# An encoder layer in float32: the vector engine's order of work in the embedding stage and at the end

## The chip, the cores and the metric

The kernel runs on one core of a Trainium2 chip. The core has a matrix engine (TensorE, PE in the profile; its weight loads are PEld), three engines for elementwise work (VectorE or DVE, ScalarE or ACT, GpSimd or POOL), and SyncE (SP), which here only issues transfers. Each engine takes its own instructions in its own order; semaphores order them against each other. Matrix products land in eight banks of PSUM, which DVE and ACT empty.

The metric is the device time of one execution in microseconds (us). Three runs of the kernel before gave 1199.0, 1199.45 and 1202.47 us; the median is 1199.45 us.

## The reference

One layer of a bidirectional encoder over 1024 tokens of width 1024, all in float32:

```
u      = x @ w_in
mix    = concat(retention(u), windowed_attention(u)) @ w_out
h      = LN1(ALPHA * x + mix)
ffn    = (silu(h @ w_ffn_gate) * (h @ w_ffn_up)) @ w_ffn_down
ple    = p @ w_ple_proj                      # p: 1024 x 256, an embedding per layer
out    = LN2(ALPHA * h + ffn + sigmoid(h @ w_ple_gate) * ple)
```

The part in the middle of this document is the last line's embedding term, sigmoid(h @ w_ple_gate) * ple. The part at the end is the last product of the FFN's down projection and LN2.

## The kernel before

**Products.** A float32 operand is split in two (`split`, line 70): ACT copies its rounded part (line 71), and DVE subtracts that from the operand (line 72). A product is then three matmuls (`mm3c`, lines 763 to 765; `mm3`, lines 77 to 79): high by high, high by low, low by high. The big products are done by the Strassen-Winograd scheme: 2 x 2 blocks of 512, and seven block products on sums and differences of blocks in place of eight. One block product (`product`, line 785) is 4 x 4 x 3 = 48 matmuls into four banks; with `outer` the loop over the contraction index kt is the outer one, so that all four banks are touched in turn from the start; without it, bank after bank is finished.

**The embedding stage.** The left operands of block products 5, 6, 7 and 4 are T1, T2, T3 and T4, which `t_sums` (line 995) makes out of blocks of h that are themselves kept as split pairs (`HB`). Each T has two halves q, of 128 x 1024 elements. For each half, DVE makes the sum in two or three passes in place (`both`: lines 1005, 1006, 1007; `less`: lines 1011, 1012), and `put` splits it by ACT and DVE. T1 and T3 take three passes a half; T2 and T4 two, on top of the one before (T2 is made in T1's buffer, T4 in T2's). `t_sums` returns nine closures, the list `steps`. They are called between the parts of the PE program: steps[0] ahead of block product 2, steps[1] and [2] within it, [3] and [4] behind it, [5] and [6] within product 5, [7] and [8] within product 6. The order of the products is 1, 2, 5, 6, 7, 4, 3.

Product 2 completes four tiles of the first block. Behind each, `embed` (line 1051) takes the product of p with w_ple_proj into a further bank (lines 77 to 79), ACT takes the sigmoid of the gate (line 1058) into one of two buffers `sg`, DVE multiplies it by that bank (line 1059) and adds the result to the token tile (line 1061). The banks of these four small products are used again, in product 5, as its four accumulators Z. Behind product 6 and the ones after it, `add4` (line 1072) adds the finished banks to what was kept.

The order on DVE, ACT and POOL in this stage is the source order as long as `es3` is open; it is closed (line 1110) behind the fourth `embed`. From there to the FFN a planner sets the order on these three engines, by its own estimate of when each instruction could start, and it also moves such free instructions ahead of source-ordered ones. PE and SP keep source order throughout.

**The end.** The down projection is 77 units (`dunits`; ND is 77) of a block row each, by the same scheme; unit k's two operands are loaded and split some ten units ahead (`dload`, `dprep`, called by `ahead`). `d_step(k)` (line 1577) issues unit k's matmuls, empties the banks when a product is complete (`dpost`, line 1480), takes one group from the list `later` (`pop`), and then calls `ahead`. Product 3 of the second part is complete at k = 64. Then seven groups of LN2's steps for token tiles 4 to 7 go into `later`: the sums of squares on ACT (`squares`, line 1413), the power -1/2 on POOL (`rstd`, lines 1428 to 1430, and line 1449), the scaling on ACT (line 1452), gain on DVE (line 1455) and bias by an accumulating transfer (line 1456). They are taken at k = 64 to 70, ahead of the calls of `ahead` that split the operands of the last three units, 74 to 76. At k = 70 product 7 is complete; `addto` (line 1398) takes its banks, and the last product (`tail`, line 1460) goes into the same banks, one token tile after the other. From `ahead(2, 4)` on, all five engines are in source order.

Of the kernel before, what the change touches and what calls it, by code (L numbers as in the profile page):

```python
# [42 lines left out]
def layer(tc, xT, xn, w_first, w_mt, w_rv, w_out, w_pg, w_pe, pT, w_gu, w_dn,  # L43
# [26 lines left out]
    def split(raw, hi, lo):  # L70
        act.activation(hi, raw, AF.Copy)  # L71
        dve.tensor_tensor(lo, raw, hi.bitcast(F32), ALU.subtract)  # L72
# [8 lines left out]
    def behind(ins):  # L81

        tc.add_manual_dep(ins.ins, recent[0], mybir.DependencyInfo(
            mybir.DependencyClass.NoSync, mybir.DependencyReason.DATA), reason="order")
        return ins
# [40 lines left out]
    def big16(shape=(P, 2, 2, S)):  # L126
        return big.tile(list(shape), F32R, tag="H", bufs=4, name=nm("H"))
# [142 lines left out]
    later, side, ticks = [], [], [0]  # L270
# [221 lines left out]
    def span(n):  # L492
        return max(n - 1, 0), min(n + 2, NT)
# [75 lines left out]
    def put(x, o, dst):  # L569
        behind(act.activation(o[:, 0, :], x, AF.Copy))  # L570
        behind(dve.tensor_tensor(o[:, 1, :], x, o[:, 0, :].bitcast(F32), ALU.subtract))
        sp.dma_start(dst, o.bitcast(F32))
# [128 lines left out]
    with tc.manual_schedule(engines={mybir.EngineType.PE}):  # L701
# [19 lines left out]
        Y = lambda hh, k: (r.out, hh, (2 * k, 2 * k + 1))  # L721
# [30 lines left out]
    def ct(shape, tag, bufs=None, dt=F32):  # L752
        return cpool.tile(list(shape), dt, tag=tag, bufs=bufs, name=nm(tag))
# [7 lines left out]
    def mm3c(o, lh, ll, rh, rl, start, stop):  # L761

        pe.matmul(o, lh, rh, start=start, stop=False, skip_group_check=True)  # L763
        pe.matmul(o, lh, rl, start=False, stop=False, skip_group_check=True)  # L764
        pe.matmul(o, ll, rh, start=False, stop=stop, skip_group_check=True)  # L765
# [11 lines left out]
    def operands(k):  # L777
        return [fetched.pop(0) for _ in range(k)]
# [3 lines left out]
    def four(k):  # L782
        return [bank(t) for t in sets[k]]

    def product(p, banks, first, stat, side=(), outer=False):

        w = operands(4)
        for kt in range(4 if outer else 0):
            for k in range(4):
                c = slice(k * P, (k + 1) * P)  # L790
                mm3c(banks[k], stat[:, 0, kt, c], stat[:, 1, kt, c], w[kt][:, 0, :], w[kt][:, 1, :], first and kt == 0, kt == 3)
            if kt < len(side):
                side[kt]()
        for k in range(0 if outer else 4):
            c = slice(k * P, (k + 1) * P)
            for kt in range(4):
                mm3c(banks[k], stat[:, 0, kt, c], stat[:, 1, kt, c], w[kt][:, 0, :], w[kt][:, 1, :], first and kt == 0, kt == 3)
            if k < len(side):
                side[k]()
# [141 lines left out]
    Z = four("b")  # L941
# [21 lines left out]
    es3 = contextlib.ExitStack()  # L963
# [28 lines left out]
    TT = {}  # L992
    arena8 = big16((P, 8, 2, HF // 2)).bitcast(F32).rearrange("p a b c -> p a (b c)")

    def t_sums():

        for n in (1, 2, 3):
            TT[n] = big16((P, 2, 4, HF))
        hi = lambda i, j, c: HB[i, j][:, 0, c, :].bitcast(F32)
        lo = lambda i, j, c: HB[i, j][:, 1, c, :].bitcast(F32)  # L1000
        hold = {}

        def both(x, left, right, c):

            dve.tensor_tensor(x, hi(*left, c), hi(*right, c), ALU.subtract)
            dve.tensor_tensor(x, x, lo(*left, c), ALU.add)
            dve.tensor_tensor(x, x, lo(*right, c), ALU.subtract)

        def less(x, left, c):

            dve.tensor_tensor(x, hi(*left, c), x, ALU.subtract)
            dve.tensor_tensor(x, x, lo(*left, c), ALU.add)

        def put(n, x, c):
            split(x, TT[n][:, 0, c, :], TT[n][:, 1, c, :])

        def step(n, q, parts=(0, 1)):
            c = slice(2 * q, 2 * q + 2)
            if 0 not in parts:
                put(n, hold[q], c)  # L1020
                return
            if n == 1:
                hold[q] = ct([P, 2, HF], "ln", 2)
            x = hold[q] if n != 3 else arena8[:, c, :]
            if n == 3:
                both(x, (1, 1), (0, 1), c)
            elif n == 1:
                both(x, (0, 1), (0, 0), c)
            else:
                less(x, (1, 1) if n == 2 else (1, 0), c)  # L1030
            if n == 4 and q == 0:
                TT[4] = ct([P, 2, 4, HF], "h2", dt=F32R)
            if 1 in parts:
                put(n, x, c)

        return [lambda k=k: [step(1, q, (k,)) for q in range(2)] for k in range(2)] + \
            [lambda k=k: step(2, 0, (k,)) for k in range(2)] + \
            [lambda n=n, q=q: step(n, q) for n, q in ((2, 1), (3, 0), (3, 1), (4, 0), (4, 1))]

    def gate_w(p, kts=range(4)):
        for kt in kts:
            stream(pgd[p - 1, kt])
# [21 lines left out]
    def store_z(upto):  # L1066
        while len(zstores) > upto:
            zstores.pop(0)()
# [20 lines left out]
    for k in range(4, NT):  # L1089
        times_alpha(k)  # L1090
    steps = t_sums()
    steps[0]()
    w2, wpe = operands(4), operands(2)

    def first_tile(k):
        embed(k, 0, X[k], wpe, "to"[k % 2], pt[k])
        if k < 2:
            pt[k + 2] = load_p(k + 2)

    for k in range(4):  # L1100
        c = slice(k * P, (k + 1) * P)
        for kt in range(4):
            mm3c(X[k], HB[1, 0][:, 0, kt, c], HB[1, 0][:, 1, kt, c], w2[kt][:, 0, :], w2[kt][:, 1, :], False, kt == 3)
        if k:
            first_tile(k - 1)
        if k in (1, 2):
            steps[k]()
    gate_w(5, (2, 3))
    first_tile(3)
    es3.close()  # L1110
    for k in range(3, 5):
        steps[k]()
    gate_w(6)
    Z = four("b")
    product(5, Z, True, TT[1], steps[5:7], True)
    store_z(0)
    gate_w(7)
    pt = {t: load_p(t) for t in range(2)}
    Y = four("a")
    product(6, Y, True, TT[2], steps[7:9])  # L1120
    gate_w(4)
    u2 = [arena8[:, 4 + k, :] for k in range(4)]
    add4(u2, s1, Y)
# [157 lines left out]
    n = 0  # L1281
    for k, upto in enumerate((2, 4, 8, 12)):
        c = slice(k * P, (k + 1) * P)
# [95 lines left out]
    accd, R, later = [], [], []  # L1379

    def load_acc():
        accd.append(a_tile([P, D], "acc"))
        sp.dma_start(accd[-1], zd[len(accd) - 1])

    def pop():
        for f in later.pop(0):
            f()
# [172 lines left out]
    NG, ND = len(gunits), len(dunits)  # L1560
# [3 lines left out]
    def ahead(what, upto):  # L1564

        units = gunits if what == 2 else dunits
        while done[what] < min(upto, len(units)):
            units[done[what]][what % 2]()
            done[what] += 1

    def load_ln2():
        for j in range(2):
            g = ct([P, D], "u", 4)
            sp.dma_start(g, lnp[2 + j].partition_broadcast(P))
            ln2.append(g)

    def d_step(k):
        dunits[k][2]()
        dunits[k][3]()
        if later and k < ND - 6:  # L1580
            pop()
        while stores and stores[0][0] <= NG + k:
            stores.pop(0)[1]()
        pa = min(10, 5 + k // 3)
        ahead(0, k + 1 + pa + 4)
        ahead(1, k + 1 + pa)
        if k in (2, 3, 4, 5, 8, 9, 10, 11):
            load_acc()
        if k == ND - 24:
            load_ln2()  # L1590

    ET = mybir.EngineType
    with tc.manual_schedule(engines={ET.PE, ET.DVE, ET.Activation, ET.Pool, ET.SP}):
        ahead(2, 4)
        for k in range(NG):
            gunits[k][1]()
            gunits[k][2]()
            ahead(2, k + 1 + min(8, 4 + k))
            while stores and stores[0][0] <= k:
                stores.pop(0)[1]()  # L1600
            j = k + 1 - NG
            if j == -6:
                arenas_a()
                op_arena(ct([P, 4, 2, HF], "h0a", dt=F32R))
                op_arena(big16((P, 4, 2, HF)))
                op_arena(big16((P, 4, 2, HF)))
                arena("chain", ct([P, 8, HF], "h0b"), 8)
            if j == -4:
                op_arena(big16((P, 4, 2, HF)))
                arena("b", big.tile([P, 8, HF], F32, tag="H", bufs=4, name=nm("H")), 8)  # L1610
            if j >= -6:
                ahead(0, j + 7)
            if j >= -4:
                ahead(1, j + 5)
        arena("chain", ct([P, 8, HF], "h2"), 8)
        op_arena(ct([P, 4, 2, HF], "h3", dt=F32R), 4)
        rings["op"] += [ct([P, 2, HF], "u", 4, F32R) for _ in range(2)]
        for k in range(ND):
            d_step(k)
# [86 lines left out]
```

## Time and profile before

| | |
|---|---|
| median of the runs | 1199.45 us |
| the profiled execution's own time | 1199.99 us |
| its span on the core, first to last instruction | 1198.0 us |
| PE busy | 1181.0 us, 99% of the span, 5892 matmuls |
| DVE busy | 771.5 us, 64% |
| ACT busy | 542.5 us, 45% |
| POOL busy | 363.8 us, 30% |
| granted PE clock, mean | 0.998 |
| embedding stage, products 5, 6 and 7 | from about 486 to 521 us |
| last product's first matmul, last matmul | 1172.5 us, 1188.7 us |

The profile's times count from the span's start. A row of the timeline gives the start, the duration, the engine, the line, the operation, output<-inputs, and the shapes; "x2" is two instructions in one row, and a bracket at the end gives the idle time of the engine before it and what ended it. Matmuls overlap, so a matmul's duration (0.39 us) is longer than the distance to the next. A row of the waits gives the engine and line that waited, for whom, the sum, the count and the longest.

### The profile page before, as it was taken

To read this page: it belongs to the slowest core of one execution; us is meant where nothing else is said; L and a number is where in the kernel's file an instruction comes from. 1 tells how busy PE (TensorE), PEld (TensorE's weight loads), DVE (VectorE), ACT (ScalarE), POOL (GpSimd) and SP (SyncE) were. 2 spreads that over 40 slices of the span, in tenths; PEclk is the share of its full clock that TensorE was granted. 3 is DMA by queue.
4 is the path that set the end of the run, shared out by engine and by line. 5 is a ranking of instruction groups with operands and counts; after the bars stand their busy time and mean duration, and the time that the engine had idled before them with its cause. 6 is when DMAs were issued, how large, how long until landed. Compare 5 with 4: busy or idle time off the path is not lost.

```text
span 1198.0 us, 16664 instructions
## 1 busy us (share of the span) xinstructions
PE 1181.0 (99%) x5892; PEld 983.9 (82%) x5892; DVE 771.5 (64%) x1346; ACT 542.5 (45%) x1046; POOL 363.8 (30%) x342
## 2 busy tenths in 40 slices
PE   9999999999999999999999999999999999999996
PEld 7888888888888888788888888888888888888885
DVE  5654788877767788947744555545554565775668
ACT  5566238676786257203323332333322325562463
POOL 2001020202010022002756465555746342034232
PEclk9999999999999999999999999999999999999999
DMA  6335635434336864666233311332123169999977
GB/s 251 110 136 211 250 120 212 160 123 162 121 126 232 324 232 167 237 219 211 88 123 132 130 64 71 132 132 98 78 88 132 71 202 300 355 276 207 263 182 210
DMA packets 78098, 207.80 MB, mean 173 GB/s; under 512 B 9024, under 2 KB 13248, under 8 KB 78016
## 3 DMA queue, kind: packets, MB, share of 16 engines
q1 hardware_dynamic: 69376, 189.98, 44.0%
q0 software_dynamic: 8640, 16.78, 8.0%
q8 instruction: 46, 0.75, 0.2%
q14 instruction: 36, 0.29, 0.1%
HBM read 139.35 MB, written 62.13 MB: 168 GB/s over the span
## 4 chain that ended last, share of the span: by engine, by line
PE 94%; DVE 3%; ACT 1%; issue 1%; DMA 0%; POOL 0%; DVEq 0%; SPq 0%; ACTq 0%
PE bmm L77 6%; PE bt L763 6%; PE bt L764 6%; PE bt L765 6%; PE bmm L79 6%; PE bmm L78 6%; PE bs L763 6%; PE bs L764 6%; PE bs L765 6%; PE bo L763 5%; PE bo L764 5%; PE bo L765 5%; PE bmm L764 5%; PE bmm L763 5%; PE bmm L765 5%; PE bo L553 2%
## 5 line engine op out<-in xcount | busy, mean ns | idle before, releaser
L77 PE MATMUL bmm<-H,w 128*128 128x512 f32 x240 | 96.8, 403 | 0.4 <-ACT H L71 0.4
L79 PE MATMUL bmm<-H,w 128*128 128x512 f32 x240 | 94.1, 392 | 0.0
L78 PE MATMUL bmm<-H,w 128*128 128x512 f32 x240 | 93.8, 391 | 0.0
L1168 POOL TENSOR_TENSOR H<-ln 128x512 f32<-128x512 f32 x22 | 29.2, 1327 | 180.9 <-DMA ln<-in_w_gu 174.3
L1198 POOL TENSOR_TENSOR ev<-ev 128x512 f32<-128x512 f32 x33 | 54.9, 1664 | 91.2 <-DVE ev L1213 64.2
L72 DVE TENSOR_TENSOR w<-H,w 128x512 fp32r<-128x512 f32 x44 | 39.1, 889 | 63.1 <-ACT w L71 63.1
L72 DVE TENSOR_TENSOR w<-raw,w 128x512 fp32r<-128x512 f32 x56 | 45.3, 810 | 45.7 <-ACT w L71 45.2
L514 POOL COPY sc<-skb 128x1 f32<-128x1 f32 x64 | 13.0, 208 | 188.3 <-PE bt L541 149.4
L1196 ACT ACTIVATE ev<-ev 128x512 f32<-128x512 f32 x33 | 20.9, 632 | 103.5 <-DVE ev L1213 103.5
L1202 POOL TENSOR_TENSOR ev<-ev,ev 128x512 f32<-128x512 f32 x44 | 62.7, 1436 | 2.6
L72 DVE TENSOR_TENSOR u<-H,u 128x512 fp32r<-128x512 f32 x47 | 37.1, 790 | 38.9 <-ACT u L71 38.6
L77 PEld LDWEIGHTS bmm<-H,w 128*128 128x128 f32 x240 | 45.2, 188 | 10.5 <-ACT H L71 1.3
L79 PEld LDWEIGHTS bmm<-H,w 128*128 128x128 f32 x240 | 45.0, 188 | 10.0
L78 PEld LDWEIGHTS bmm<-H,w 128*128 128x128 f32 x240 | 45.1, 188 | 7.7
L71 ACT ACTIVATE u<-H 128x512 fp32r<-128x512 f32 x47 | 29.7, 631 | 43.5 <-PE bt L765 9.0
L523 ACT ACTIVATE sc<-sc,st 128x385 f32<-128x385 f32 (+1 forms) x64 | 37.2, 584 | 25.3 <-DVE st L521 25.2
L519 DVE CUSTOM_DVE_ANT_0 sc<-cst,bs,skb 128x384 f32<-128x384 f32 (+1 forms) x64 | 34.9, 576 | 16.3 <-PE bs L518 15.7
L71 ACT ACTIVATE w<-raw 128x512 fp32r<-128x512 f32 x56 | 34.7, 624 | 17.1 <-PE bo L79 7.0
L475 POOL TENSOR_TENSOR sm<-sm,cst 128x8 f32<-128x8 f32 x8 | 15.6, 1950 | 86.9 <-DVE sm L474 86.9
L874 POOL TENSOR_TENSOR stt<-stt,cst 128x1 f32<-128x1 f32 x8 | 12.1, 1514 | 91.2 <-DVE stt L873 91.2
L1172 POOL TENSOR_TENSOR H<-raw,H 128x512 f32<-128x512 f32 x22 | 37.8, 1718 | 0.0
L71 ACT ACTIVATE w<-H 128x512 fp32r<-128x512 f32 x44 | 27.4, 622 | 21.4 <-PE bs L765 6.3
(802 smaller groups left out, 3822.6 us busy)
## 6 DMA issues: line engine op xcount, KB each, us to landing
ad<-ev SPq DMA_DIRECT2D x33, 512.0 KB, 2.7
pgd<-pro SPq DMA_DIRECT2D x28, 512.0 KB, 2.8
raw<-in_w_gu SPq DMA_DIRECT2D x22, 512.0 KB, 4.3
ln<-in_w_gu SPq DMA_DIRECT2D x22, 512.0 KB, 3.5
raw<-ad SPq DMA_DIRECT2D x40, 256.0 KB, 5.5
ln<-ad SPq DMA_DIRECT2D x37, 256.0 KB, 6.7
H<-in_w_dn SPq DMA_DIRECT2D x33, 256.0 KB, 7.7
wod<-aq SPq DMA_DIRECT2D x15, 512.0 KB, 2.6
```

The lines of the kernel that those rows point to most:

```text
L71: act.activation(hi, raw, AF.Copy)
L72: dve.tensor_tensor(lo, raw, hi.bitcast(F32), ALU.subtract)
L77: pe.matmul(o, lh, rh, start=start, stop=False)
L78: pe.matmul(o, lh, rl, start=False, stop=False)
L79: recent[0] = pe.matmul(o, ll, rh, start=False, stop=stop).ins.name
L523: act.activation(sc[g][:, :nk + 1], sc[g][:, :nk + 1], AF.Exp, bias=st_[:, 1, j, g:g + 1], accum_out=st_[:, 2, j, g:g + 1])
L763: pe.matmul(o, lh, rh, start=start, stop=False, skip_group_check=True)
L764: pe.matmul(o, lh, rl, start=False, stop=False, skip_group_check=True)
L765: pe.matmul(o, ll, rh, start=False, stop=stop, skip_group_check=True)
L1172: pool.tensor_tensor(s[3], a(0, 1), s[0], ALU.subtract)
L1198: pool.tensor_tensor(c[:, 1, :], c[:, 0, :], c[:, 1, :], ALU.mult)
L1202: pool.tensor_tensor(self.ev[dst][:, 0, :], left, right, op)
```

## The change

In the embedding stage the closures of `t_sums` become eight, two for each T: `sums` makes the passes of both halves, `parts` splits both. steps[0] stands where it stood, steps[1] too; T2's sums and splits come behind the fourth `embed`, T3's within product 5, and T4's within product 6. `es3` is closed behind product 6. At the end, `d_step` takes a group of LN2's steps behind its calls of `ahead` for k = 64 to 70, and ahead of them for smaller k as before.

```
-        return [lambda k=k: [step(1, q, (k,)) for q in range(2)] for k in range(2)] + \
-            [lambda k=k: step(2, 0, (k,)) for k in range(2)] + \
-            [lambda n=n, q=q: step(n, q) for n, q in ((2, 1), (3, 0), (3, 1), (4, 0), (4, 1))]
+        return [lambda f=f, n=n: [f(n, q) for q in range(2)] for n in (1, 2, 3, 4) for f in (sums, parts)]
...
-        if k in (1, 2):
-            steps[k]()
+        if k == 1:
+            steps[1]()
     gate_w(5, (2, 3))
     first_tile(3)
-    es3.close()
-    for k in range(3, 5):
+    for k in range(2, 4):
         steps[k]()
     gate_w(6)
     Z = four("b")
-    product(5, Z, True, TT[1], steps[5:7], True)
+    product(5, Z, True, TT[1], steps[4:6], True)
     store_z(0)
     gate_w(7)
     pt = {t: load_p(t) for t in range(2)}
     Y = four("a")
-    product(6, Y, True, TT[2], steps[7:9])
+    product(6, Y, True, TT[2], steps[6:8])
+    es3.close()
...
     def d_step(k):
         dunits[k][2]()
         dunits[k][3]()
-        if later and k < ND - 6:
+        if later and k < ND - 13:
             pop()
         while stores and stores[0][0] <= NG + k:
             stores.pop(0)[1]()
         pa = min(10, 5 + k // 3)
         ahead(0, k + 1 + pa + 4)
         ahead(1, k + 1 + pa)
+        if later and ND - 13 <= k < ND - 6:
+            pop()
```

The orders of PE, SP and POOL are the same in both programs, and so is the number of instructions on each engine. On DVE about thirty instructions of the embedding stage and two pairs at the end stand elsewhere, on ACT five instructions at the end, and the two halves of T2's split change places.

In the changed kernel DVE takes, behind T1's splits: the second, third and fourth multiply and add of `embed`, T2's two passes on the first half and two on the second, T2's two splits, five passes of T3, the first bank of `add4`, T3's sixth pass, T3's first split, the second bank, T3's second split, and T4 with the third and fourth banks between its passes. At the end the splits of unit 75 stand ahead of the sums of squares of tile 5, and those of unit 76 ahead of the scaling of tile 4.

More of the change, by code (lines that the diff above doesn't have):

```diff
@@ L1015, in put, with span, sums @@
             split(x, TT[n][:, 0, c, :], TT[n][:, 1, c, :])
[L1017 to L1021, printed above, removed]
+        def span(q):
+            return slice(2 * q, 2 * q + 2)
+        def sums(n, q):
+            c = span(q)
             if n == 1:
@@ L1030, in step, with parts @@
                 less(x, (1, 1) if n == 2 else (1, 0), c)
+        def parts(n, q):
             if n == 4 and q == 0:
                 TT[4] = ct([P, 2, 4, HF], "h2", dt=F32R)
-            if 1 in parts:
-                put(n, x, c)
-        return [lambda k=k: [step(1, q, (k,)) for q in range(2)] for k in range(2)] + \
-            [lambda k=k: step(2, 0, (k,)) for k in range(2)] + \
-            [lambda n=n, q=q: step(n, q) for n, q in ((2, 1), (3, 0), (3, 1), (4, 0), (4, 1))]
+            put(n, hold[q] if n != 3 else arena8[:, span(q), :], span(q))
+        return [lambda f=f, n=n: [f(n, q) for q in range(2)] for n in (1, 2, 3, 4) for f in (sums, parts)]
     def gate_w(p, kts=range(4)):
```

## The prediction

> **What bounds the kernel now.** First the page, then the waits of PE, then the timelines of PE, DVE, ACT and POOL around the waits that the change can reach. The page's head and the waits of PE:
>
> ```profile
> span 1198.0 us, 16664 instructions
> ...
> PE 1181.0 (99%) x5892; PEld 983.9 (82%) x5892; DVE 771.5 (64%) x1346; ACT 542.5 (45%) x1046; POOL 363.8 (30%) x342
> ...
> PE bmm L763 <- DVE sg L1059: 1.8, 1, 1.8
> ...
> PE bo L763 <- DVE sg L1059: 0.7, 1, 0.7
> PE bs L763 <- DVE acc L1398: 0.6, 1, 0.6
> ```
>
> PE is the bound; only what lets it wait less, or more, changes the time. Three of its waits lie where the edit is: two for the third and fourth multiply of `embed` (line 1059), one for the emptying of a bank ahead of the last product (line 1398). PE in the embedding stage:
>
> ```profile
> 485.49 0.39 PE L79 MATMUL bo<-u,p 128*128 128x512 f32 x1
> 485.71 0.39 PE L763 MATMUL bmm<-w,H 128*128 128x512 f32 x1
> ...
> 488.32 0.50 PE L763 MATMUL bmm<-w,H 128*128 128x512 f32 x1 [1.77 <-DVE sg L1059]
> ...
> 490.65 0.50 PE L763 MATMUL bo<-w,H 128*128 128x512 f32 x1 [0.67 <-DVE sg L1059]
> ...
> 491.45 0.39 PE L763 MATMUL bmm<-u,H 128*128 128x512 f32 x1
> ...
> 499.61 0.39 PE L763 MATMUL bt<-w,H 128*128 128x512 f32 x1
> ...
> 510.49 0.39 PE L763 MATMUL bt<-w,H 128*128 128x512 f32 x1
> ```
>
> Product 5 starts at 485.71, product 6 at 499.61, product 7 at 510.49. The last two are 48 matmuls apart: 10.88 / 48 = 0.2267 us each where nothing waits. Product 5's first 12 matmuls should end at 485.71 + 12 x 0.2267 = 488.43; the thirteenth starts at 491.45. The two waits with their slow restarts cost 3.02 us. What DVE and ACT do then:
>
> ```profile
> 470.94 1.22 DVE L1005 TENSOR_TENSOR ln<-h,h0a 128x1024 f32<-128x1024 f32 x1
> 472.19 1.23 DVE L1006 TENSOR_TENSOR ln<-ln,h 128x1024 f32<-128x1024 f32 x1
> ...
> 481.85 0.68 DVE L1059 TENSOR_TENSOR sg<-sg,bo 128x512 f32<-128x512 f32 x1
> 482.44 1.22 DVE L1011 TENSOR_TENSOR ln<-h,ln 128x1024 f32<-128x1024 f32 x1
> 483.58 0.68 DVE L1061 TENSOR_TENSOR acc<-acc,sg 128x512 f32<-128x512 f32 x1
> ...
> 485.32 2.35 DVE L1012 TENSOR_TENSOR ln<-ln,h 128x1024 f32<-128x1024 f32 x2
> 487.59 0.68 DVE L1059 TENSOR_TENSOR sg<-sg,bmm 128x512 f32<-128x512 f32 x1
> ...
> 484.35 0.60 ACT L1058 ACTIVATE sg<-bs 128x512 f32<-128x512 f32 x1 [3.96 <-DVE acc L1061]
> 486.56 2.19 ACT L71 ACTIVATE H<-ln 128x1024 fp32r<-128x1024 f32 x2 [1.61 <-DVE ln L1012]
> ```
>
> The third multiply starts at 487.59, after four passes of T2 (lines 1011, 1012), though T2 is not wanted before 499.61. The fourth small product's last matmul ends by 485.49 + 0.39 = 485.88; the fourth sigmoid waited for the second add (line 1061), itself behind a T2 pass. Now the end:
>
> ```profile
> 1171.48 0.39 PE L765 MATMUL bmm<-H 128*128 128x512 f32 x1
> 1172.51 0.47 PE L763 MATMUL bs<-H 128*128 128x512 f32 x1 [0.64 <-DVE acc L1398]
> ...
> 1160.49 0.62 ACT L71 ACTIVATE h<-raw 128x512 fp32r<-128x512 f32 x1
> ...
> 1164.37 1.24 ACT L1452 ACTIVATE acc<-acc,stt 128x1024 f32<-128x1024 f32 x1 [0.28 <-POOL stt L1449]
> 1165.52 0.71 ACT L1413 ACTIVATE sg<-acc,stt 128x512 f32<-128x512 f32 x1
> ...
> 1166.93 0.62 ACT L71 ACTIVATE u<-ln 128x512 fp32r<-128x512 f32 x1
> ...
> 1162.70 0.20 DVE L1428 TENSOR_SCALAR stt<-stt 128x1 f32<-128x1 f32 x1
> ...
> 1167.58 0.69 DVE L72 TENSOR_TENSOR u<-ln,u 128x512 fp32r<-128x512 f32 x1 [2.38 <-ACT u L71]
> ...
> 1168.79 1.22 DVE L1455 TENSOR_TENSOR acc<-acc,u 128x1024 f32<-128x1024 f32 x1
> ...
> 1171.68 1.28 DVE L1398 TENSOR_TENSOR acc<-acc,bs 128x512 f32<-128x512 f32 x2
> ...
> 1189.13 0.69 DVE L1398 TENSOR_TENSOR acc<-acc,bmm 128x512 f32<-128x512 f32 x1 [0.18 <-PE bmm L765]
> ...
> 1157.02 0.86 POOL L1340 DMA_DIRECT2D h<-in_w_dn  x1 [0.41 <-DVE H L72]
> 1163.18 0.56 POOL L1430 TENSOR_TENSOR stt<-stt,cst 128x1 f32<-128x1 f32 x1 [5.30 <-DVE stt L1429]
> 1163.82 0.52 POOL L1449 TENSOR_TENSOR stt<-stt 128x1 f32<-128x1 f32 x1
> ...
> 1165.91 0.19 POOL L1449 TENSOR_TENSOR stt<-stt 128x1 f32<-128x1 f32 x1
> ```
>
> Without the wait the last product would start at 1171.48 + 0.23 = 1171.71; it starts at 1172.51, and 0.08 later again by its slow restart (0.47 instead of 0.39). The end is worth 0.88 us at most. After it DVE waits for PE at 1189.13: what PE gains there the end of the span gains.
>
> **The change part by part.** *Third and fourth multiply ahead of T2.* Nothing is added or removed; DVE's order changes. The second multiply stays at 481.85, its add follows at 482.44 + 0.1 (it depends on it), done by 483.2; so the fourth sigmoid can run at about 483.2 (its bank is complete by then: the next small product follows it on PE), done by 483.9 in place of 484.95. The third small product ends about 6 x 0.2267 = 1.36 before the fourth, at 484.5: third multiply 484.6 to 485.3, its add to 486.0, fourth multiply 486.0 to 486.7, its add to 487.4. Product 5 wants the third one's bank for its second accumulator at 485.71 + 3 x 0.2267 = 486.39 and the fourth one's for its fourth at 487.75. Both are there 1.1 us early. PE gains all of the 3.02 us.
>
> *T2 later.* Two passes, then two: the rows of lines 1005 and 1006 are 1.25 apart where one needs the other, the pair on line 1012, independent, 2.35 - 1.22 = 1.13. From 487.3: 1.25 + 1.13 + 1.25 + 1.13 gives 492.1; ACT splits the second half by 492.1 + 1.1 = 493.2, DVE by 494.5. Product 6 now starts at 499.61 - 3.02 = 496.59. Slack 2.1 us, so no cost; all beyond it would be PE's. [...]
>
> *T3 and T4, and the banks between them.* From 494.4, five passes of T3 end at 500.4. Then DVE must take product 6's first bank, complete at 496.59 + 2.72 + 0.2 = 499.5: no wait. Sixth pass, first split, second bank (complete 502.2), second split: 505.1, against product 7 at 510.49 - 3.02 = 507.47. If PE were later here, the banks would be later, but never so late that product 7 waits: the second bank comes half a product ahead of it, and 0.6 + 1.2 us of DVE follow. T4 with banks three and four ends near 513.7, product 4 starts at 518.35. Cost nothing.
>
> *Queues.* ACT holds only the splits here; POOL nothing. SP's order is kept, and its stores of the tiles can go earlier, since the adds do. Product 6's last weights:
>
> ```profile
> 485.91 0.42 SPq L774 DMA_DIRECT2D u<-pgd  x1
> ...
> DMA to landing us min/median/max: 2.6/4.0/7.5
> ```
>
> At the longest landing of these transfers 485.91 + 7.5 = 493.4, ahead of 496.59. From here on every stage is paced by PE or by what PE frees, so I let the 3.02 us travel to the end unshortened.
>
> *The end: splits of units 75 and 76 ahead of LN2's steps.* Same instructions, other order on ACT and DVE. ACT: 0.52 for a split's copy (1160.49 to the next), 1.41 for a pair of squares (1165.52 to 1166.93), 1.15 for a scaling (1164.37 to 1165.52). Unit 74's copies end at 1161.5, unit 75's at 1162.6, squares of tile 5 at 1164.0, unit 76's copies at 1165.1. DVE takes unit 75's halves to 1163.9, and only then tile 4's small steps, 1162.70 before: 1.2 later. POOL then needs 0.56 + 0.52 + gaps: tile 4's scaling starts at 1165.5 in place of 1164.37. But unit 76 is out of the way: scaling to 1166.7, squares of tile 6 to 1168.1, scaling of tile 5 to 1169.3, squares of tile 7 to 1170.7; then DVE's two small steps, and line 1398 at 1171.1 in place of 1171.68. That is 0.6 of the 0.88. Bounds: all of it, 0.88, if a step or two is quicker; below nothing, -0.4, if POOL's steps lose a further microsecond to DVE's splits. I take 0.6, since every step has its own row. Unit 76's accumulating transfer was issued at 1157.02; its copy is now wanted at 1164.5, 7.5 us later:
>
> ```profile
> DMA to landing us min/median/max: 4.5/4.8/7.1
> ```
>
> *Sum.* Span 1198.0 - 3.02 - 0.6 = 1194.4. The profiled execution took 1199.99, so 1.99 lie around the span: 1196.4. The median of the runs is 0.54 below the profiled one: 1195.85, against 1199.45.
>
> **The rivals.** *B: POOL eats the end's gain.* The row at 1163.82 took 0.52, the same step at 1165.91 took 0.19. DVE was subtracting in a split at the first and idle at the second. In the new order tile 4's power follows unit 75's splits and precedes unit 76's by 0.3 us; if DVE gets in first, power and product lose between 0.33 (0.52 - 0.19, one of them) and 0.66 (both), ACT's whole chain slips by some 0.5, and line 1398 is back at 1171.6. Then only 3.02 + 0.1 is left: 1196.3. For it: the two rows; against it: the power should start while DVE waits for ACT. [...]
>
> *C: T2 comes late.* If DVE's chain behind the fourth multiply runs 3.6 us longer than I reckon, PE waits 1.5 at product 6: 1.5 + 0.6 are left, 1197.3. For it: T2 had 7 us of slack and keeps 2.1. Against it: no DVE duration in the rows varies by more than 0.1 us.
>
> *D: slower.* T2 now stands behind two multiplies that wait for PE, ACT and the transfers of p. If the fourth small product is late, PE waits for it in either kernel, but here the sums wait too. From 2.1 us of lateness this costs, from 2.1 + 3.6 = 5.7 the kernel is slower than before, and with 9.3 by 0.3%, 1203. The trace shows no such wait of PE at 484.35 to 485.49, which speaks against it.
>
> **How the numbers follow.** Chances: forecast 0.65, B 0.17, C 0.10, D 0.08. 0.3% is 3.6 us, about what a measurement of this kernel can tell from no change, and the forecast's 3.6 lies on it; its own range is 1195.2 to 1196.6 with the runs' scatter of half a microsecond. I count 0.7 of the forecast and a quarter of B as over 0.3% (0.50), D as slower (0.08), the rest as within (0.42). Range: down to the full 3.9 with 0.9 of scatter below, 1194.6; up past B and most of C, 1198.6.
>
> **What would show it.** Right: no PE wait for line 1059, product 6 starting 10.9 us after product 5, no PE wait on T2 (lines 71, 72) at product 6 or on line 1072 at 7; the third multiply within 0.2 us of its small product's end; the wait for line 1398 at 0.3 or less. Wrong: a PE wait of over half a microsecond at product 6, 7 or 4; new PE waits in the FFN or the down projection, which would mean that the shift is absorbed there; a wait for line 1398 of 0.6 or more (B).

## The result, and the profile after

The changed kernel took 1195.99 us (median of 6 runs, 1194.9 to 1196.8), against 1199.62 us for the kernel before beside it (6 runs). The ratio is 0.9966 with a 95% interval of 0.9953 to 0.9979, so the gain is 3.6 us, 0.2 to 0.5%. The forecast was 1195.85. The profiled span fell from 1198.0 to 1194.4 us, the forecast's own figure.

The head of the page of the changed kernel, and its waits of PE (us in total, times, longest). Line numbers behind the embedding's function are one lower than before: 1059 is now 1058, 1398 is 1397.

```profile
span 1194.4 us, 16665 instructions
...
PE 1180.5 (99%) x5892; PEld 984.2 (82%) x5892; DVE 773.2 (65%) x1346; ACT 542.6 (45%) x1046; POOL 366.3 (31%) x342
...
PE bt L404 <- ACT ptr L543: 1.6, 1, 1.6
...
PE bt L763 <- DMA u<-wod: 0.3, 1, 0.3
PE bs L763 <- DVE acc L1397: 0.2, 1, 0.2
```

The two waits for `embed`'s multiply are gone; the one at the end is 0.2 in place of 0.6; the longest that is left (line 404) lies in an earlier stage. PE has as many instructions as before and as much busy time within 0.5 us: all that changed is what it waits. The timeline of PE in the embedding stage and at the end, changed kernel:

```profile
485.88 0.39 PE L763 MATMUL bmm<-w,H 128*128 128x512 f32 x1
...
496.76 0.39 PE L763 MATMUL bt<-w,H 128*128 128x512 f32 x1
...
507.64 0.39 PE L763 MATMUL bt<-w,H 128*128 128x512 f32 x1
...
518.52 0.39 PE L763 MATMUL bt<-w,h 128*128 128x512 f32 x1
...
1168.37 0.39 PE L765 MATMUL bmm<-H 128*128 128x512 f32 x1
1168.94 0.47 PE L763 MATMUL bs<-H 128*128 128x512 f32 x1 [0.18 <-DVE acc L1397]
```

Products 5, 6, 7 and 4 start 10.88 us apart each: 48 matmuls without a gap. Before, product 6 came 13.90 behind product 5, so the embedding stage gives 3.02 us. At the end PE lost 1168.94 - 1168.37 - 0.23 = 0.34 us, against 1172.51 - 1171.48 - 0.23 = 0.80 before: 0.46 less. The last product starts 1172.51 - 1168.94 = 3.57 earlier: 3.02 and 0.46, and 0.24 for matmuls between 994.65 and 995.34 that were slow in the trace of before alone, less 0.17 by which product 5 starts later (485.88 against 485.71); that makes 3.55, to 0.02.

DVE in the changed kernel, from the second multiply to T3's last split:

```profile
482.02 0.68 DVE L1058 TENSOR_TENSOR sg<-sg,bo 128x512 f32<-128x512 f32 x1
...
484.79 0.69 DVE L1058 TENSOR_TENSOR sg<-sg,bmm 128x512 f32<-128x512 f32 x1 [1.36 <-PE bmm L79]
...
487.48 1.22 DVE L1011 TENSOR_TENSOR ln<-h,ln 128x1024 f32<-128x1024 f32 x1
...
492.27 2.44 DVE L72 TENSOR_TENSOR H<-ln,H 128x1024 fp32r<-128x1024 f32 x2
...
500.67 0.68 DVE L1071 TENSOR_TENSOR H<-raw,bt 128x512 f32<-128x512 f32 x1
...
504.14 1.22 DVE L72 TENSOR_TENSOR H<-H,H 128x1024 fp32r<-128x1024 f32 x1
```

The third multiply now waits for its small product (1.36 us idle, released by line 79), where before it stood behind T2's passes. T2 is ready at 492.27 + 2.44 = 494.71, 2.05 ahead of product 6; T3 at 505.36, 2.28 ahead of product 7.

### The profile page after: what moved, and what is told of

Same layout as the page of the kernel before. It is cut to its first block, busy times and chain, and to the rows that moved or that the text cites. A ratio compares the mean times of both kernels' runs of the same rounds, so it can differ in the third digit from the quotient of the medians.

```text
span 1194.4 us, 16665 instructions
## 1 busy us (share of the span) xinstructions
PE 1180.5 (99%) x5892; PEld 984.2 (82%) x5892; DVE 773.2 (65%) x1346; ACT 542.6 (45%) x1046; POOL 366.3 (31%) x342
## 4 chain that ended last, share of the span: by engine, by line
PE 96%; ACT 1%; DVE 1%; DMA 1%; issue 0%; POOL 0%; SPq 0%; DVEq 0%; ACTq 0%
PE bmm L77 6%; PE bt L763 6%; PE bt L765 6%; PE bt L764 6%; PE bs L763 6%; PE bs L765 6%; PE bs L764 6%; PE bmm L79 6%; PE bmm L78 6%; PE bmm L765 5%; PE bmm L763 5%; PE bo L765 5%; PE bo L763 5%; PE bo L764 5%; PE bmm L764 5%; PE bo L553 2%
```

## The experiments

**The changed kernel once more (e0), and each half alone (e1, e2).** e0 is the changed kernel. e1 has the embedding's edit and `d_step` as before; e2 has `d_step` as changed and the embedding as before:

```
 def d_step(k):                       # e1 against the changed kernel
-        if later and k < ND - 13:
+        if later and k < ND - 6:
             pop()
...
-        if later and ND - 13 <= k < ND - 6:
-            pop()
```

> The changed kernel once more, as the measure for the three kernels beside it. Both theories expect what its first profile showed: 3.6 us less than before, no PE wait in products 5 to 7, and a wait of 0.2 us for line 1397 ahead of the last product.

> The embedding stage's half of the change alone; the end as before. Theory (two separate terms: a bank that DVE gives back in time in product 5, and DVE's chain ahead of the last product): 3.0 us less than before, the PE waits for line 1058 gone, the wait for the bank ahead of the last product at 0.6 us and more, as before. Rival (part of the gain is a shift that the transfer-bound down projection gives to the end): the end's wait shrinks here too, and the gain is nearer 3.6.

> The end's half alone; the embedding stage as before. Theory: 0.4 to 0.6 us less than before, from the wait ahead of the last product, 0.64 to 0.2; the two waits in product 5 stay at 1.8 and 0.7. Rival (the end's order has no effect, POOL's slow steps take it back): 0.0 to 0.1 less, and the wait stays at 0.6.

Measured, each against the kernel before on the same chip (1200.04): e0 1196.67, ratio 0.9974 [0.9963, 0.9984]; e1 1196.41, ratio 0.9973 [0.9961, 0.9985], span 1194.6; e2 1199.99, ratio 1.0000 [0.9991, 1.0008], span 1197.7. The waits of PE in e2:

```profile
PE bmm L763 <- DVE sg L1059: 1.7, 1, 1.7
...
PE bo L763 <- DVE sg L1059: 0.7, 1, 0.7
```

All of the gain that can be measured is the embedding's; the end alone shows none. e1 brought the very numbers of its rival (3.63 us less and no wait at the end). But the rival's reason, a shift given on by the embedding, doesn't fit e2, which has the embedding as before and no wait at the end either. No line of e2's list has the wait for the emptying of the bank. It is missing from e0's too, which has the same order at the end and should have shown 0.2, and from e1's, which has the old one and should have shown 0.6. So whether PE waits there is not a matter of the order of LN2's steps alone.

**The squares ahead (e3).** The groups of LN2's steps are dealt out anew, on top of the changed kernel (q squares, f power, m scaling, w gain and bias; indices 0 to 3 are tiles 4 to 7): tile 7's squares go ahead of tile 5's scaling, and tile 5's gain behind the emptying of the banks:

```
-  [w[0], m[1], q[3], f[2]], [w[1], m[2], f[3]], [m[3]], [w[2], w[3]]
+  [w[0], q[3], f[2], m[1]], [m[2], f[3]], [m[3]], [w[1], w[2], w[3]]
```

> The changed kernel with another order of the last norm steps: the squares of tile 7 ahead of the scaling of tile 5, and DVE's gain pass of tile 5 behind the last product's four bank reads. Theory (what is left of the wait is ACT's chain, scaling, squares, scaling, squares, ahead of DVE's small step for tile 7): line 1397 starts about 1 us earlier, PE's wait there is gone, 0.4 us less than the changed kernel, and POOL's steps for tiles 6 and 7, 1.93 and 1.01 us beside DVE's gain passes, fall towards 0.6 and 0.2. Rival (DVE is late again, now in the last product, because three gain passes stand ahead of it): the same time as the changed kernel, the wait moved to line 1395 or 1434.

Measured: 1196.81, ratio 0.9976 [0.9967, 0.9985], span 1196.8, no better than e0, with a wait of 1.4 us where none was expected. The profiled execution is the slowest of e3's ten (1198.83 us), so such a wait is not in all of them. The timeline of DVE in e3 around the end, then PE's wait:

```profile
1158.40 0.68 DVE L1395 CUSTOM_DVE_ANT_0 acc<-acc,bo 128x512 f32<-128x512 f32 x1
...
1170.14 1.27 DVE L1397 TENSOR_TENSOR acc<-acc,bs 128x512 f32<-128x512 f32 x2
...
1169.21 0.39 PE L765 MATMUL bmm<-H 128*128 128x512 f32 x1
1170.96 0.47 PE L763 MATMUL bs<-H 128*128 128x512 f32 x1 [1.36 <-ACT acc L1451]
```

The work from the first custom pass on the preceding product's banks (line 1395, at 1158.40) to the emptying (1170.14) is a fixed chain on DVE, ACT and POOL: here 11.74 us. The same two rows give its length in every profile. PE restarts 0.82 after the emptying begins (1170.96 - 1170.14). What varies is the lead, the time from that first pass to the moment at which PE would be free for the last product (here 1169.21 + 0.23 - 1158.40 = 11.04). In the kernel before, DVE's first pass of the chain is this row; its emptying (1171.68) and PE's last matmul ahead of it (1171.48) stand in the prediction:

```profile
1158.09 0.68 DVE L1396 CUSTOM_DVE_ANT_0 acc<-acc,bo 128x512 f32<-128x512 f32 x1
```

PE waits where the chain plus 0.82 is longer than the lead (us, from the same rows of each trace; e4 to e8 follow below):

| kernel | order at the end | chain | lead | PE waits |
|---|---|---|---|---|
| before | old | 13.59 | 13.62 | 0.80 |
| e1 | old | 13.60 | 15.15 | 0 |
| after | new | 12.92 | 13.40 | 0.34 |
| e0 | new | 12.94 | 15.39 | 0 |
| e2 | new | 12.92 | 14.92 | 0 |
| e4 | new | 12.92 | 13.97 | 0 |
| e5 | new | 12.93 | 13.49 | 0.26 |
| e6 | new | 12.92 | 12.06 | 1.69 |
| e7 | new | 12.92 | 14.74 | 0 |
| e8 | new | 12.93 | 14.85 | 0 |
| e3 | squares first | 11.74 | 11.04 | 1.52 |

The edit at the end makes the chain 0.67 us shorter each time, and e3's order another 1.18. But the lead varies by 4.3 us between traces, without regard to the order. What starts the chain is seen on ACT ahead of it. The timeline of ACT in e3 and, below it, in e0:

```profile
1157.12 0.63 ACT L71 ACTIVATE H<-h0b 128x512 fp32r<-128x512 f32 x1 [0.55 <-DMA h0b<-in_w_dn]
```

```profile
1151.88 0.63 ACT L71 ACTIVATE H<-h0b 128x512 fp32r<-128x512 f32 x1 [1.15 <-DMA h0b<-in_w_dn]
```

The split just ahead of the chain waits for an accumulating transfer of `w_dn` to land: in all eleven traces it starts 0.104 or 0.105 us after one has landed (e3: landed at 1157.015). With the old order PE needs a lead of 13.59 + 0.83 = 14.42. Six of the eleven traces have less; over all eleven the edit would save 0.35 us on average (0.67 in five, 0.45 in e4, nothing in five), 0.03% of the time. That is below what e2's interval can resolve. Why the transfers land earlier in one run than in another stays open.

**The source order given up, in two places (e4, e5).** `es3.close()` is where the planner takes over. e4 closes it behind `first_tile(3)`, where it stood before, e5 behind T2:

```
     first_tile(3)
+    es3.close()                      # e4
     for k in range(2, 4):
         steps[k]()
+    es3.close()                      # e5
...
     product(6, Y, True, TT[2], steps[6:8])
-    es3.close()                      # both
```

> The changed kernel, but the source order of DVE, ACT and POOL ends behind the fourth embedding tile, where it ended before; the planner then puts three of T2's four passes back between the multiplies and adds. Theory (the bank's multiply must not stand behind sums): the third multiply is just in time, the fourth ends near 488.5, PE wants its bank at 487.9 and waits 0.6 to 0.7 with a slow restart: 0.6 to 0.9 us more than the changed kernel. Rival (the grouping of sums and splits by itself makes the gain): the same time as the changed kernel, no PE wait in product 5.

> The changed kernel, but source order ends behind T2's splits: T3, T4 and the sums of banks are the planner's again, with two T3 and T4 passes in another order. Theory (T3 and T4 have slack, their order is free): the same time as the changed kernel within 0.2 us, no PE wait in products 5 to 7. Rival (source order to the sixth product is part of the gain): 0.5 us or more is lost in product 7 or 4.

Measured: e4 1197.13, ratio 0.9971 [0.9960, 0.9983], span 1194.1; e5 1200.05, ratio 0.9997 [0.9988, 1.0005], span 1198.4. In e4 the planner puts T2's passes between the multiplies again; the third multiply is in time, and PE loses 0.65 us at the fourth one, as expected; the time doesn't show it. The waits of PE in e4, then DVE's emptying of product 6's first bank:

```profile
PE bo L763 <- DVE sg L1058: 0.4, 1, 0.4
```

```profile
504.00 0.68 DVE L1071 TENSOR_TENSOR H<-raw,bt 128x512 f32<-128x512 f32 x1
```

T3, T4 and the banks are the planner's in e4 too, and no later product waits. So 3.02 - 0.65 = 2.4 us of the embedding's gain come without the edit to `es3.close()`. e5 is the miss: I had taken the order of T3 and T4 for free, and the whole gain is lost. DVE and ACT in e5 ahead of product 7:

```profile
498.96 1.22 DVE L1011 TENSOR_TENSOR ln<-h0b,ln 128x1024 f32<-128x1024 f32 x1
...
503.50 1.22 DVE L1012 TENSOR_TENSOR ln<-ln,h0b 128x1024 f32<-128x1024 f32 x1
504.64 1.22 DVE L1011 TENSOR_TENSOR ln<-h0b,ln 128x1024 f32<-128x1024 f32 x1
505.78 1.22 DVE L72 TENSOR_TENSOR H<-H,H 128x1024 fp32r<-128x1024 f32 x1
506.91 1.22 DVE L1012 TENSOR_TENSOR ln<-ln,h0b 128x1024 f32<-128x1024 f32 x1
508.05 1.22 DVE L72 TENSOR_TENSOR h<-ln,h 128x1024 fp32r<-128x1024 f32 x1
509.18 0.68 DVE L1071 TENSOR_TENSOR H<-raw,bt 128x512 f32<-128x512 f32 x1
...
508.16 1.06 ACT L71 ACTIVATE h<-ln 128x1024 fp32r<-128x1024 f32 x1 [2.28 <-DVE ln L1012]
```

T3 is ready in time (last split 505.78 + 1.22 = 507.00). But the planner puts T4's passes (lines 1011, 1012 on `h0b`) among T3's and T4's first split ahead of the emptying of product 6's first bank (line 1071): 509.18, against 500.67 in the changed kernel. Product 7 goes into that bank, and DVE works on sums that nobody wants for 10 us. PE in e5, and below it the windows view (stretch, its length, then busy us and count of PE, weight load, DVE, ACT, POOL, then the granted clock, DMA share and GB/s):

```profile
507.42 0.39 PE L765 MATMUL bs<-u,H 128*128 128x512 f32 x1
509.96 0.47 PE L763 MATMUL bt<-w,H 128*128 128x512 f32 x1 [2.16 <-ACT h L71]
...
511.33 0.63 PE L765 MATMUL bt<-u,H 128*128 128x512 f32 x1
511.76 0.63 PE L763 MATMUL bt<-w,H 128*128 128x512 f32 x1
```

```profile
511.00:514.00 3.00, 3.00 (x9) 2.33 (x8) 1.79 (x3) 0.00 (x0) 0.00 (x0) 0.50 0.71 289
```

The page names ACT's line 71 as releaser. That instruction ended at 509.22 and writes T4, which product 7 doesn't read; the emptying ended at 509.86, and PE starts at 509.96. The wait costs 509.96 - 507.42 - 0.23 = 2.31. A microsecond later the granted clock is 0.50 and matmuls come 0.42 to 0.43 apart for 3.4 us: another 1.60, with 0.10 for the slow restart ahead of it. Together that is the 4.0 us by which e5's span is longer than the changed kernel's. e4 had the planner too, and no such order; so what costs is the order that the planner chose from this point on, not that it chose.

**Extra work ahead of T2 (e6, e7).** Three, or six, additional DVE passes of 128x1024, into a buffer that T3 overwrites later, stand behind `first_tile(3)`; they are work that the kernel doesn't need:

```
     first_tile(3)
+    for k in range(3):               # e6; range(6) in e7
+        dve.tensor_tensor(<T3's buffer>, <high part>, <low part>, ALU.add)
     for k in range(2, 4):
```

> The changed kernel with three further DVE passes of 128 x 1024, into a part that T3's sums overwrite, between the fourth add and T2: T2 comes 3.5 us later. As the prediction had it (slack 2.1 us against product 6's first matmul): PE waits 1.4 us at product 6. Other theory (the first matmul that needs T2's low part is the third, the first that needs its second half the seventh; by the profile the slack is 3.5 and 3.9): 0 to 0.2 us, the same time as the changed kernel within 0.3.

> The same with six passes, T2 7.0 us later. As the prediction had it: 4.9 us of PE waits. Other theory: product 6's third matmul waits 3.3 us for the first half's low part, and T3, which the banks of product 6 now stand between, costs product 7 up to 0.9: 3.3 to 4.5 us more than the changed kernel, so slower than before or equal to it.

Measured: e6 1196.71, ratio 0.9970 [0.9961, 0.9980], no wait of PE in the embedding stage. e7: 1202.44, ratio 1.0017 [1.0008, 1.0026]. DVE and PE in e6, then PE in e7, at the start of product 6:

```profile
487.97 3.49 DVE L1110 TENSOR_TENSOR H<-h0a 128x1024 f32<-128x1024 f32 x3
...
496.17 2.44 DVE L72 TENSOR_TENSOR H<-ln,H 128x1024 fp32r<-128x1024 f32 x2
...
497.25 0.39 PE L763 MATMUL bt<-w,H 128*128 128x512 f32 x1
...
497.70 0.39 PE L765 MATMUL bt<-w,H 128*128 128x512 f32 x1
```

```profile
497.16 0.39 PE L765 MATMUL bo<-u,H 128*128 128x512 f32 x1
498.54 0.50 PE L763 MATMUL bt<-w,H 128*128 128x512 f32 x1 [0.99 <-ACT H L71]
498.88 0.40 PE L764 MATMUL bt<-w,H 128*128 128x512 f32 x1
500.98 0.50 PE L765 MATMUL bt<-w,H 128*128 128x512 f32 x1 [1.71 <-DVE H L72]
...
502.55 0.63 PE L764 MATMUL bt<-w,H 128*128 128x512 f32 x1
```

In e6 T2 is complete at 496.17 + 2.44 = 498.61, 1.36 after product 6 has begun, and nobody waits. e7's two waits tell why: the first two matmuls of a product want only ACT's rounded part of T2 (line 71); the third (line 765) is the first to want DVE's remainder, of the first half alone; the second half comes from the seventh on. So the slack is read at the third matmul. In the changed kernel the remainder of the first half is there at 492.27 + 1.22 = 493.49, the third matmul at 496.76 + 2 x 0.227 = 497.21: 3.7 us. In e6 that remainder is there at 497.39, 0.31 ahead of its matmul at 497.70; three passes fit, just. In e7 the waits cost 1.15 + 1.87 us, and again the clock drops, for another 1.60. So e7 took 5.7 us more than e6, where 3.3 to 4.5 more than the changed kernel were expected: the slow clock was in neither theory. Windows view of e7:

```profile
501.00:505.00 4.00, 4.00 (x11) 3.19 (x12) 3.57 (x4) 0.00 (x0) 0.00 (x0) 0.61 0.31 105
```

**Passes and splits by halves again (e8).** What is left of the embedding's edit is the order of passes and splits. e8 takes it back for T2, T3 and T4; the place behind the fourth `embed` and the source order stay:

```
-  [lambda f=f, n=n: [f(n, q) for q in range(2)] for n in (1, 2, 3, 4) for f in (sums, parts)]
+  [lambda f=f: [f(1, q) for q in range(2)] for f in (sums, parts)] + \
+      [lambda n=n, q=q: [f(n, q) for f in (sums, parts)] for n in (2, 3, 4) for q in range(2)]
```

> The changed kernel with one part taken back: T2, T3 and T4 are again worked by halves (passes on the first half, its split, passes on the second half, its split); the place of T2 behind the fourth embed and the source order to the sixth product stay. Nothing of the computation is left out. My theory: what gave the 3 us is that embed's adds no longer stand behind T2's splits, and that stays; T2 becomes ready up to 1 us later or earlier than 494.7, which the slack at product 6 (at least 3.5 us by the run with three more passes) covers; T3 by halves waits for the scalar engine's rounded half between its passes, some 1 us later, within the 2.2 us between T3's readiness (505.36) and product 7 (507.64) unless that wait comes twice. So no wait of TensorE at products 5 and 6, at most 0.5 us at product 7, span 1194 to 1195, time 1196 to 1197. Rival (the order of passes ahead of splits is itself part of the gain): a wait of TensorE of 1 us or more at product 6 or 7, perhaps with the half clock behind it, span 1196 or more, time 1198 to 1200.

Measured: 1198.36 against 1200.61, ratio 0.9980 [0.9971, 0.9988], span 1195.5: by the medians a third of the gain is gone, though the interval still overlaps that of e0; the trace is what shows the loss. DVE in e8 at T2's first half, then the waits of PE in e8:

```profile
488.81 1.23 DVE L1012 TENSOR_TENSOR ln<-ln,h 128x1024 f32<-128x1024 f32 x1
491.16 1.23 DVE L72 TENSOR_TENSOR H<-ln,H 128x1024 fp32r<-128x1024 f32 x1 [1.13 <-ACT H L71]
```

```profile
PE bt L765 <- DVE H L72: 0.4, 1, 0.4
...
PE bs L763 <- DVE H L1072: 0.3, 1, 0.3
```

Each half's split leaves DVE idle for 1.13 us, until ACT has rounded that half. T2 is complete at 497.13 (its second half's split starts at 495.90), 2.4 later than in the changed kernel where I had expected 1 at most, at no cost; T3 is then late too, and PE waits at product 7 and product 4. With the slow restarts that is 0.72 + 0.52 = 1.24 us; the span is 1.1 longer. My theory had the first wait but not the second; the rival's wait of over 1 us at one place did not come. Product 5 has no wait in e8: its 3.02 us come from T2's passes and splits no longer standing ahead of the multiplies (in e4 three of the four passes stand there again, the splits don't, and 0.65 is lost). What the halves take back, 1.24, they take at products 7 and 4; T2, T3 and T4 were changed together, so the share of each is not shown.

## Why the prediction was right

- *Embedding, 3.02 us for PE.* Right: both waits went, product 6 starts 10.88 behind product 5, the third multiply starts at 484.79 where 484.6 was reckoned. e1 shows that this half carries the measured gain, e2 that without it there is none.
- *T2 ready at 494.5, slack 2.1.* The time was right (494.71), the slack mis-sized: it was measured against product 6's first matmul, though the first two read only ACT's part: it is 3.7 us, which e6 and e7 enclose. In the kernel before, T2's last split ended at 491.73, 7.9 ahead of product 6's first matmul, where the prediction says 7. So C needed more lateness than I gave it; once it is there it costs more, because a slow clock follows (1.60 us on top of the waits in e7).
- *Dependent passes 1.25 apart, independent ones 1.13.* Held: 487.48 to 488.73 is 1.25, 488.73 to 489.88 is 1.15.
- *T3, T4 and the banks cost nothing.* Right for the order written in the source (T3 at 505.36 where 505.1 was reckoned), but I gave it as a matter of slack, and it is a matter of order: in the order that the planner chose in e5 product 6's banks are emptied late, for 2.31 us and a slow clock behind it; by halves (e8) it costs 1.24. The prediction named neither the edit to `es3.close()` nor the order of passes and splits as a term of the sum. The order of passes and splits protects the gain. By the traces the edit to `es3.close()` is worth 0.65 against the place where it stood (e4), and 4.0 against a place behind T2 (e5).
- *"I let the 3.02 us travel to the end unshortened."* In the two profiles of the prediction it did. It need not: at the end PE can wait for the chain whose start is set by transfers, and e6, which has the embedding of the changed kernel at no cost, lost 1.69 us there.
- *The end, 0.6 of 0.88.* The mechanism was right: the chain of steps is 0.67 shorter in every trace. Its worth was mis-sized, because I took the wait in one trace as a property of the kernel. Where the lead is over 14.42 us there is nothing to gain; over eleven traces the step is worth about 0.35 us, and no run measures it. That the sum 3.02 + 0.6 met the median to 0.14 us is therefore partly chance: e1 has 3.63 us without the second term, e0 3.37 with it, both with some 1.5 us either way. That the span met 1194.4 to the tenth is chance as well: the end gave 0.46 in place of 0.6, and the 0.24 of slow matmuls and the 0.17 of the later start were in no sum.
- *B, POOL.* The interference is there, but off the path, as this timeline of POOL in the changed kernel shows, with DVE's passes on the tile beside it:

```profile
1164.07 1.01 POOL L1448 TENSOR_TENSOR stt<-stt 128x1 f32<-128x1 f32 x1
...
1166.09 1.93 POOL L1429 TENSOR_TENSOR stt<-stt,cst 128x1 f32<-128x1 f32 x1
...
1163.80 1.23 DVE L1454 TENSOR_TENSOR acc<-acc,u 128x1024 f32<-128x1024 f32 x1 [0.45 <-ACT acc L1451]
1166.39 1.23 DVE L1454 TENSOR_TENSOR acc<-acc,u 128x1024 f32<-128x1024 f32 x1 [0.78 <-ACT acc L1451]
```

The product at 1164.07 took 1.01 in place of 0.19 (at 1165.91 in the kernel before, where DVE is idle) and ends at 1165.08, 0.05 after DVE's pass; ACT was free for it at 1165.11. The power at 1166.09 took 1.93 in place of 0.56 (at 1165.28 in the kernel before, where DVE is idle); ACT waited 0.55 for it at 1168.32, when the emptying had begun at 1168.12. The first row looks as if the product had waited for the pass. The second doesn't settle it: the power starts 0.30 ahead of DVE's pass, and directly behind a transfer that POOL issues, where a power without such a pass beside it took 0.85 (at 1173.48 in the kernel before). So about 1.1 us go with the pass, and which of the two was first can't be read.

D did not come: no small product was late.

## What to carry to other kernels

Where DVE's queue holds work for a distant consumer ahead of work that PE wants next, read how late the nearer piece may be and put the distant one behind it; then check each later hand-over in the same order, since a planner that is let in again may spend the gain. For a split operand, measure slack against the first instruction that reads each part, not against the first that reads any. A wait that one trace shows behind a transfer should be looked for in several traces before it is put into a sum.

## What the runs showed of the hardware

A wait of PE can cost more than its length. In e5 one gap of 2.31 us, and in e7 gaps of 1.15 and 1.87 with two matmuls between them, were followed within about a microsecond by 3.4 us at half clock (granted 0.50 from 511.0 to 514.4 in e5, from 501.9 to 505.3 in e7), in which matmuls came 0.42 to 0.43 apart in place of 0.227: 1.60 us more each time. The kernel before lost 1.92 and 0.84 us in product 5, six matmuls apart, with no such drop in its trace; windows view of the kernel before, where the granted clock is 1.00, as it is from 491 to 500:

```profile
486.00:491.00 5.00, 2.56 (x11) 1.49 (x10) 5.00 (x7) 2.12 (x2) 0.00 (x0) 1.00 0.99 367
```

Nor did the single gaps of 1.5 to 1.7 us at the end of e3 and e6 lower it (granted 1.00 from 1171 to 1175 in both).

What makes the drop follow one gap and not another, these traces don't show. Nor does the drop seem to come in every execution: of e5's twelve, four show a mean clock of 0.998 and took 1198.4 to 1199.3 us, six show 0.996 and took 1199.9 to 1202.3, and two, the profiled one among them, show 0.997 and took 1199.9 and 1200.5.
